# Seven products in place of eight for the second half of two squared-ReLU layers, and for three of four pairs of the first half

## The chip, the cores and the metric

The program runs on one core of one Trainium2 chip. The metric is the device time of one execution in microseconds (us). TensorE (PE in the rows; PEld is its weight loads) multiplies, VectorE (DVE), ScalarE (ACT) and GpSimd (POOL) do elementwise work, and SyncE (SP) issues the loads of weights.

## The reference, cut to what matters

Two blocks run one after the other on 512 tokens of 1024 channels, in float32. The first block is a gated delta rule with a SwiGLU layer, the second has two layers of attention, each followed by

```python
def sq_relu_mlp(x, w1, w2):
    h = jax.nn.relu(x @ w1)
    return (h * h) @ w2          # D_MODEL 1024, D_FF_2 4096

h = h + sq_relu_mlp(rms_norm(h, mlp_norm[i]), mlp_w1[i], mlp_w2[i])    # i = 0, 1
```

The change is in these two layers (`mlp`, called here mlp 0 and mlp 1). The SwiGLU layer (`w_gate_up` and `w_down`, 2816 wide) shares a helper with them.

## The kernel before

Everything is kept transposed: 128 channels on the partitions, tokens along the row. mlp 0 has 528 tokens, mlp 1 has 512; a half is 264 or 256. A product in float32 is made from three matmuls of split operands: high by high, high by low, low by high. Each weight tile `wr` is loaded by SP, copied to `wh` by ScalarE and subtracted to `wl` by VectorE; the splitting costs the two engines one instruction each.

**The helper `seven` (L104)** multiplies a 2x2 arrangement of weights by a 2x2 arrangement of operands with seven block products in place of eight. Four quarters of a pair of weight blocks arrive by four loads (L118 to L121); VectorE makes two sums of 128x512 (L122, L123) and GpSimd two more (L124, L125); the seven combinations are split in four groups (L130, L131: three of 128x1024, one of 128x512), and each product is 12 matmuls (L138), 84 in all. An object `evac` takes the results out of PSUM. The order is product 11, s2, s3, s1, 12, s4, 22; the last one adds to the bank of s3 after `out22` has read it.

**`mlp` (L1614)** works in four parts (`CHUNKS`) of eight feature blocks of 128. In a part, four pairs of feature blocks are made: in the first part two pairs by plain products (96 matmuls a pair), two by `seven`, in the later parts all four by `seven`, with `Squares` as evac. The features are ReLU, square and split to `fh` and `fl` (L177, L178). Then `down` (L1084) makes the eight output blocks by plain products of 8 blocks each (L1098) and `add` multiplies each result by the row of inverse norms `rs` and adds it to `h` (L1655, L1656). In mlp 0 `down` uses two halves of 264 columns, in mlp 1 one piece of 512. `operand_sums` (L1583) makes the summed operands t1 to t4 for the sevens in the first part.

**SwiGLU** uses `seven` for most of its second half, with the class `Adds` (L982) as evac: two runs of four sevens, and in each seven three of the six results go to `h` by a GpSimd addition (L1005, L1009, L1013).

Order is set by a scheduler that walks all instructions by priority and by its own estimate of time; each engine then runs its list in order, with semaphores between engines. A tile of a pool with `bufs=n` has n slots under its tag; a slot is free when everything that touches the tile in it is done. In `seven`, `wr` of g1 and g3 come from a pool with three slots (shared with the plain weights), g2 and g4 from another with two; `wh` and `wl` have two slots in each pool. PSUM has eight banks for `pd` in `mlp`.

## Time and profile before

| What | Value |
|---|---|
| median of 3 runs | 2571.34 us (2569.33 to 2573.19) |
| the profiled execution, its own time | 2559.74 us |
| its span | 2558.0 us |
| mean granted TensorE clock | 0.986 |
| busy share PE, DVE, ACT, POOL | 96%, 71%, 47%, 24% |

The time is that of the whole execution; the span runs from the first instruction to the last and is 1.74 us shorter. Matmuls are pipelined, so the busy share of PE counts their overlapping spans and is no measure of speed; the number of matmuls in a window is.

### The profile page before, as it was taken

What the parts mean: (1) busy time and instruction counts of PE and PEld (TensorE: products, weight loads), DVE (VectorE), ACT (ScalarE), POOL (GpSimd) and SP (SyncE); (2) the same over time, 40 slices, a digit from 0 to 9 for tenths busy, and PEclk for the clock granted to TensorE, in tenths of its full rate; (3) what the DMA queues carried; (4) which work ended last, traced back from release to release, by engine and by line L of the source; (5) the groups of instructions that cost most, each with busy time, mean ns of one, the idle gap of its engine ahead of it and who ended that gap; (6) DMA issues with size and microseconds to landing.
All of it is one profiled execution on the core that took longest, in us unless ns stands there. A gap on an engine that the chain in (4) does not pass through costs nothing.

```text
span 2558.0 us, 48433 instructions
## 1 busy us (share of the span) xinstructions
PE 2452.0 (96%) x18732; PEld 2306.2 (90%) x18732; DVE 1807.8 (71%) x3766; ACT 1203.1 (47%) x2419; POOL 607.5 (24%) x751
## 2 busy tenths in 40 slices
PE   8899999999999999999887999999999999999999
PEld 8899999999899888888887999999999999788987
DVE  7878877856654576655999667676764878866764
ACT  5434445343423333335455664543634767634543
POOL 2332222100001123232671220121121444301210
PEclk9999999999999999999998999999999999999999
DMA  4334342434563323233331323323333322223322
GB/s 155 96 98 106 86 115 80 110 96 117 173 231 96 91 78 112 85 95 108 93 77 34 94 92 95 104 79 96 119 106 92 106 64 75 86 94 107 104 90 92
DMA packets 150741, 257.36 MB, mean 101 GB/s; under 512 B 66816, under 2 KB 70944, under 8 KB 150512
## 3 DMA queue, kind: packets, MB, share of 16 engines
q1 hardware_dynamic: 93696, 236.47, 30.3%
q10 hardware_dynamic: 56816, 17.82, 3.6%
q8 instruction: 147, 2.41, 0.4%
q14 instruction: 82, 0.67, 0.1%
HBM read 223.39 MB, written 22.34 MB: 96 GB/s over the span
## 4 chain that ended last, share of the span: by engine, by line
PE 70%; DVE 15%; DMA 8%; ACT 3%; issue 3%; POOL 1%; SPq 0%; ACTq 0%; DVEq 0%; POOLq 0%
PE ps_pd L100 33%; PE ps_pd L1098 15%; PE ps_pd L138 8%; DMA wr<-wm 3%; DVE wl L131 2%; DVE wl L84 1%; PE ps_pa L1501 1%; PE ps_po L1945 1%; PE ps_pb L733 1%; DMA wd<-Xt 1%; DVE prod L910 1%; PE ps_pt L1934 1%; DVE sc L1430 1%; ACT wh L83 1%; DVE sc L1418 1%
## 5 line engine op out<-in xcount | busy, mean ns | idle before, releaser
L100 PE MATMUL ps_pd<-bigh,wh 128*128 128x256 f32 (+5 forms) x2256 | 693.6, 309 | 16.7 <-ACT bigh L180 6.4
L100 PE MATMUL ps_pd<-bigh,wl 128*128 128x256 f32 (+5 forms) x2256 | 691.6, 308 | 4.3 <-DVE wl L84 4.3
L100 PE MATMUL ps_pd<-bigl,wh 128*128 128x256 f32 (+5 forms) x2256 | 690.7, 307 | 0.9 <-DVE bigl L181 0.8
L83 ACT ACTIVATE wh<-wr 128x1024 fp32r<-128x1024 f32 (+3 forms) x295 | 302.7, 1027 | 549.6 <-PE ps_pd L100 230.8
L100 PEld LDWEIGHTS ps_pd<-bigh,wh 128*128 128x128 f32 (+1 forms) x2256 | 429.6, 191 | 37.9 <-ACT bigh L180 6.4
L100 PEld LDWEIGHTS ps_pd<-bigh,wl 128*128 128x128 f32 (+1 forms) x2256 | 429.3, 191 | 22.2 <-DVE wl L84 5.3
L100 PEld LDWEIGHTS ps_pd<-bigl,wh 128*128 128x128 f32 (+1 forms) x2256 | 429.2, 190 | 19.2 <-DVE bigl L181 1.6
L84 DVE TENSOR_TENSOR wl<-wr,wh 128x1024 fp32r<-128x1024 f32 (+3 forms) x283 | 348.1, 1230 | 88.6 <-ACT wh L83 83.8
L1098 PE MATMUL ps_pd<-fh,wh 128*128 128x264 f32 (+1 forms) x816 | 262.0, 326 | 1.9 <-ACT wh L83 1.8
L1098 PE MATMUL ps_pd<-fl,wh 128*128 128x264 f32 (+1 forms) x816 | 262.9, 325 | 0.0
L1098 PE MATMUL ps_pd<-fh,wl 128*128 128x264 f32 (+1 forms) x816 | 261.8, 326 | 0.1
L130 ACT ACTIVATE wh<-wr 128x1024 fp32r<-128x1024 f32 (+1 forms) x144 | 134.8, 950 | 179.2 <-DVE wr L123 67.5
L131 DVE TENSOR_TENSOR wl<-wr,wh 128x1024 fp32r<-128x1024 f32 (+1 forms) x144 | 177.5, 1244 | 13.2 <-ACT wh L130 12.3
L1098 PEld LDWEIGHTS ps_pd<-fh,wh 128*128 128x128 f32 x816 | 152.5, 188 | 17.1 <-ACT wh L83 4.5
L1098 PEld LDWEIGHTS ps_pd<-fh,wl 128*128 128x128 f32 x816 | 152.8, 188 | 13.6 <-DVE wl L84 0.6
L1098 PEld LDWEIGHTS ps_pd<-fl,wh 128*128 128x128 f32 x816 | 153.2, 188 | 13.0
L124 POOL TENSOR_TENSOR wr<-wr 128x512 f32<-128x512 f32 x36 | 58.2, 1617 | 437.4 <-DVE wr L122 256.9
L138 PE MATMUL ps_pd<-bigh,wh 128*128 128x264 f32 (+1 forms) x448 | 125.8, 285 | 5.9 <-DVE u L1563 4.3
L138 PE MATMUL ps_pd<-bigl,wh 128*128 128x264 f32 (+1 forms) x448 | 125.2, 283 | 1.2 <-DVE bigl L1594 1.2
L138 PE MATMUL ps_pd<-bigh,wl 128*128 128x264 f32 (+1 forms) x448 | 123.8, 282 | 0.0
L1655 DVE TENSOR_TENSOR y<-ps_pd,rrow 128x264 f32<-128x264 f32 (+1 forms) x96 | 49.1, 515 | 101.3 <-PE ps_pd L1098 95.2
L100 PE MATMUL ps_pd<-xh,wh 128*128 128x264 f32 (+1 forms) x400 | 116.3, 293 | 0.3 <-ACT t L1824 0.3
(517 smaller groups left out, 5881.9 us busy)
## 6 DMA issues: line engine op xcount, KB each, us to landing
wr<-w SPq DMA_DIRECT2D x72, 512.0 KB
wr<-wm SPq DMA_DIRECT2D x128, 256.0 KB
wr<-wm SPq DMA_DIRECT2D x64, 512.0 KB
wr<-wgu SPq DMA_DIRECT2D x44, 512.0 KB
wr<-wa SPq DMA_DIRECT2D x17, 512.0 KB
wr<-wkv SPq DMA_DIRECT2D x17, 512.0 KB
wr<-wdq SPq DMA_DIRECT2D x32, 256.0 KB
wr<-wao SPq DMA_DIRECT2D x16, 512.0 KB
```

The lines of the kernel that those rows point to most:

```text
L83: nc.scalar.activation(wh, wr, AF.Copy)
L84: (self.low or nc.vector).tensor_tensor(wl, wr, wh, ALU.subtract)
L100: nc.tensor.matmul(ps[:, :half], a[:, k], b[k][:, ts], start=(k == 0 and i == 0), stop=(k == kt - 1 and i == 2))
L124: nc.gpsimd.tensor_tensor(g1[:, 1], g2[:, 0], g4[:, 0], ALU.add)
L130: nc.scalar.activation(wh[:, : kq * m], v, AF.Copy)
L131: nc.vector.tensor_tensor(wl[:, : kq * m], v, wh[:, : kq * m], ALU.subtract)
L138: nc.tensor.matmul(ps, a[:, q], c[q], start=(start and q == 0 and i == 0), stop=(q == kq - 1 and i == 2), skip_group_check=not start,)
L733: nc.tensor.matmul(pq[r, c, :w], lhs(pr)[:, c], rhs(pr)[:, c], start=True, stop=True)
L910: nc.vector.tensor_tensor(prod[:, :i, :i], X[:, :i, :i], bt[:, :i, i].rearrange("p (o j) -> p o j", o=1).broadcast_to([2 * H, i, i]), ALU.mult
L1098: nc.tensor.matmul(pss[h][:, :half], a[:, q], b[f0 + q][:, ts], start=(f0 + q == 0 and i == 0), stop=(f0 + q == nf - 1 and i == 2),)
L1418: nc.vector.scalar_tensor_tensor(acc[:n, c0:c1], rl[:n, : c1 - c0], wi[:n, i, hd : hd + 1], acc[:n, c0:c1], ALU.mult, ALU.add)
L1655: nc.vector.tensor_tensor(y, ps, norm["rs"][:, t], ALU.mult)
```

## The change

The second half of both layers goes through `seven` too (16 calls in each `mlp`, with `Adds`), and in the three later parts the fourth pair of features is made by plain products. Since the operands of the second half now need sums of features, a class `Features` keeps seven blocks of half the tokens for a pair, `u`, and makes three differences and sums on VectorE. `h` is multiplied by the mean square (`inv`) in the first part and by the inverse (`rs`) in the last; the results of a product go into `h` without the norm row in between. For the first two outputs of a part `seven` runs with `last`: five products take their first three feature pairs before the fourth is needed. The slots move: g1, g3 and g4 come from the pool with three, g2 from a pool with one; the split of g4 has a tag of its own. The scratch tiles p1, u2 and w of `mlp` come from the tags `sq` and `acc` with two slots each, and so do those of `operand_sums`.

```diff
     def seven(self, wdram, x, n, evac, last=False):
-        pools = (self.wp, self.wq, self.wp, self.wq)
-        g1, g2, g3, g4 = (
-            p.tile([128, 2, 512], F32, name="wr", tag="wr", bufs=self.wr_bufs - (p is self.wq))[:, :, : kq * 128] for p in pools
-        )
+        def quarters(p, bufs):
+            return p.tile([128, 2, 512], F32, name="wr", tag="wr", bufs=bufs)[:, :, : kq * 128]
+
+        g1, g3, g4 = (quarters(self.wp, self.wr_bufs) for _ in range(3))
+        g2 = quarters(self.wq, 1)
...
+        both = ("wh", "wl")
+        groups = (
+            (("11", "s2"), (g1, 2, self.wp, both, self.ws_bufs)),
+            (("s3", "s1"), (g2, 2, self.wq, both, 1)),
+            (("12", "s4"), (g3, 2, self.wp, both, self.ws_bufs)),
+            (("22",), (g4, 1, self.wq, ("w3h", "w3l"), 1)),
+        )
...
+        tail = range(kq)
+        if last:
+            z = bank()
+            tail = range(kq - 1, kq)
+            for i in range(3):
+                weights(i)
+            for ps, w, b in ((x1, "11", "b11"), (u, "s2", "t2"), (y, "s3", "t3"), (v, "s1", "t1"), (z, "s4", "b22")):
+                product(ps, q[w], b, qs=range(kq - 1))
...
 class Adds:
-    def __init__(self, k, s, h, j, lo, half):
+    def __init__(self, k, scratch, h, j, lo, half, eng=None):
         self.k, self.nc, self.half = k, k.nc, half
-        self.p1, self.u2, self.w = (s.tile([128, half], F32, name=x, bufs=2) for x in ("p1", "u2", "w"))
+        self.eng = eng or k.nc.gpsimd
+        self.p1, self.u2, self.w = (scratch(x)[:, :half] for x in ("p1", "u2", "w"))
...
+class Features:
+    SLOTS = ("b11", "t3", "b21", "b22", "t1", "t2", "t4")
+    def __init__(self, k, s, m):
+        self.k, self.nc = k, k.nc
+        self.u = s.tile([128, 7, T // 2], F32, name="u", bufs=1)[:, :, :m]
+        self.parts = [s.tile([128, 7, T // 2], F32R, name=x, bufs=FPAIRS)[:, :, :m] for x in ("fh", "fl")]
...
+    def done(self, i):
+        k, nc, u, (hi, lw) = self.k, self.nc, self.u, self.parts
+        v = self.block(i)
+        nc.scalar.activation(v, v, AF.Square)
+        if i == 0:
+            k.split(hi[:, 0], lw[:, 0], u[:, 0])
+            nc.vector.tensor_tensor(u[:, 4], u[:, 0], u[:, 1], ALU.subtract)
+        else:
+            nc.vector.tensor_tensor(u[:, 1], u[:, 3], u[:, 1], ALU.subtract)
+            nc.vector.tensor_tensor(u[:, 5], u[:, 4], u[:, 3], ALU.add)
+            nc.vector.tensor_tensor(u[:, 6], u[:, 5], u[:, 2], ALU.subtract)
+            k.split(hi[:, 1:], lw[:, 1:], u[:, 1:])
...
 def operand_sums(k, h, x, norm, lo, n, i, scratch):
-    g22 = pool.tile([128, T // 2], F32, name="g22", tag="fh", bufs=RING)[:, :m]
+    g22 = scratch("p1")[:, :m]
...
 def mlp(k, io, h, i, before, lo=0, n=T):
+        def scratch(name):
+            if name == "w":
+                return k.sm.tile([128, 640], F32, name="w", tag="acc", bufs=2)
+            return k.sm.tile([128, T], F32, name=name, tag="sq", bufs=2)
...
         for c in range(CHUNKS):
+            fs = []
+            for j in range(part // 2):
+                w = w1[(i * nf + c * part) // 2 + j]
+                fs.append(Features(k, s, m))
+                if j in MIX[min(c, 1)]:
+                    k.seven(w, x, n, Squares(k, scratch, m, fs[-1]))
                 else:
+                    plain(w, fs[-1])
...
+                row("inv", k.sm.tile([128, T], F32, name="inv", tag="sq", bufs=2), ms)
+            y = {c: tuple([f.parts[e][:, a] for f in fs] for e in range(2)) for a, c in enumerate(Features.SLOTS)}
+            for j in range(0, 8, 2):
+                v = h[:, j : j + 2, tokens]
+                if c == 0:
+                    nc.gpsimd.tensor_tensor(v, v, rows["inv"].rearrange("p (o t) -> p o t", o=1).broadcast_to(list(v.shape)), ALU.mult)
+                end = c == CHUNKS - 1
+                late = end and j == 6
+                k.seven(w2[i, j // 2, c], y, n, Adds(k, scratch, h, j, lo, m, nc.vector if late else None), j == 0)
...
+                if end:
+                    for a in range(2):
+                        (nc.vector if late else nc.gpsimd).tensor_tensor(v[:, a], v[:, a], rows["rs"], ALU.mult)
+
+MIX = ((2, 3), (0, 1, 2))
+FPAIRS = 4
...
-RING = 10
```

## Rows read from the trace of the kernel before

**Rows 1.** The page: span, and busy us (share) xinstructions of each engine.

```profile
span 2558.0 us, 48433 instructions
PE 2452.0 (96%) x18732; PEld 2306.2 (90%) x18732; DVE 1807.8 (71%) x3766; ACT 1203.1 (47%) x2419; POOL 607.5 (24%) x751
```

**Rows 2.** Windows at full pace: SwiGLU sevens, mlp 0 `down`, mlp 1 `down`.

```profile
1080.00:1090.00 10.00, 10.00 (x87) 10.00 (x86) 6.14 (x11) 3.00 (x4) 6.00 (x4) 1.00 0.38 107
...
1680.00:1700.00 20.00, 20.00 (x166) 20.00 (x165) 14.87 (x22) 6.09 (x7) 4.31 (x3) 1.00 0.25 83
...
2360.00:2380.00 20.00, 20.00 (x88) 16.28 (x87) 13.42 (x16) 4.77 (x5) 4.71 (x3) 1.00 0.20 66
```

**Rows 3.** Windows: first part, later parts of mlp 0 and 1, one SwiGLU seven.

```profile
1529.60:1603.00 73.40, 71.28 (x570) 69.80 (x569) 54.71 (x104) 31.80 (x54) 7.15 (x4) 1.00 0.28 88
...
1732.50:1821.20 88.70, 88.45 (x723) 88.03 (x722) 62.08 (x93) 39.18 (x56) 14.64 (x8) 1.00 0.29 90
...
2420.60:2506.60 86.00, 84.74 (x531) 75.78 (x530) 57.62 (x77) 38.89 (x56) 14.19 (x8) 1.00 0.29 92
...
959.70:971.20 11.50, 10.20 (x85) 10.03 (x85) 9.43 (x12) 4.04 (x6) 8.60 (x6) 1.00 0.39 115
```

**Rows 4.** PE's waits (us, times, longest): SwiGLU sevens, mlp 0, mlp 1.

```profile
PE ps_pd L138 <- DVE p L1004: 4.7, 3, 1.9
...
PE ps_pd L138 <- DVE u L1563: 1.5, 3, 0.8
...
PE ps_pd L138 <- DVE u L1563: 2.8, 3, 1.1
```

**Rows 5.** Groups of VectorE by shape in mlp 0: busy us, mean ns.

```profile
L131 DVE TENSOR_TENSOR wl<-wr,wh 128x1024 fp32r<-128x1024 f32 x41 | 57.2, 1406 | 5.9 <-ACT wh L130 5.3
...
L178 DVE TENSOR_TENSOR fl<-u,fh 128x528 fp32r<-128x528 f32 x30 | 22.2, 740 | 15.6 <-ACT fh L177 15.5
...
L123 DVE TENSOR_TENSOR wr<-wr 128x512 f32<-128x512 f32 x13 | 9.0, 691 | 7.2 <-DMA wr<-wm 7.0
L122 DVE TENSOR_TENSOR wr<-wr 128x512 f32<-128x512 f32 x13 | 8.9, 688 | 12.5 <-DMA wr<-wm 12.2
L131 DVE TENSOR_TENSOR wl<-wr,wh 128x512 fp32r<-128x512 f32 x13 | 8.8, 678 | 0.0
...
L1563 DVE TENSOR_TENSOR u<-ps_pd,w 128x264 f32<-128x264 f32 x14 | 6.0, 431 | 0.4
...
L1594 DVE TENSOR_TENSOR bigl<-gt,bigh 128x264 fp32r<-128x264 f32 x8 | 3.1, 418 | 0.0
```

**Rows 6.** Timeline of VectorE in a SwiGLU seven (start us, us).

```profile
969.65 0.69 DVE L123 TENSOR_TENSOR wr<-wr 128x512 f32<-128x512 f32 x1 [1.88 <-DMA wr<-wdq]
...
975.27 1.43 DVE L131 TENSOR_TENSOR wl<-wr,wh 128x1024 fp32r<-128x1024 f32 x1
...
976.96 0.89 DVE L131 TENSOR_TENSOR wl<-wr,wh 128x512 fp32r<-128x512 f32 x1
```

**Rows 7.** Timeline of SP's issues in the same stretch: g4 of two sevens.

```profile
966.32 0.33 SPq L119 DMA_DIRECT2D wr<-wdq  x1
...
977.88 0.33 SPq L119 DMA_DIRECT2D wr<-wdq  x1
```

**Rows 8.** Timelines: VectorE and GpSimd, overlapping and alone.

```profile
1621.25 3.46 DVE L131 TENSOR_TENSOR wl<-wr,wh 128x1024 fp32r<-128x1024 f32 x2 [0.38 <-ACT wh L130]
...
1624.97 1.21 DVE L131 TENSOR_TENSOR wl<-wr,wh 128x1024 fp32r<-128x1024 f32 x1
...
1592.21 1.29 POOL L125 TENSOR_TENSOR wr<-wr 128x512 f32<-128x512 f32 x1 [4.77 <-DMA wr<-wm]
...
1621.30 2.33 POOL L125 TENSOR_TENSOR wr<-wr 128x512 f32<-128x512 f32 x1
...
982.06 0.74 POOL L1009 TENSOR_TENSOR h<-h,w 128x256 f32<-128x256 f32 x1 [0.70 <-DVE w L1008]
```

**Rows 9.** Timeline of VectorE at the end of the span.

```profile
2554.20 0.69 DVE L1656 TENSOR_TENSOR h<-h,y 128x512 f32<-128x512 f32 x1
```

More of the change, by code (lines that the diff above doesn't have):

```diff
@@ L101, in products, with seven @@
             evac(ps[:, :half], slice(h * half, (h + 1) * half))
-    def seven(self, wdram, x, n, evac):
+    def seven(self, wdram, x, n, evac, last=False):
         nc = self.nc
@@ L132, in part, with product @@
             return [(wh[:, kq * i : kq * i + kq], wl[:, kq * i : kq * i + kq]) for i in range(m)]
-        def product(ps, w, b, start=True):
+        def product(ps, w, b, start=True, qs=range(kq)):
             (wh, wl), (bh, bl) = w, x[b]
-            for q in range(kq):
+            for q in qs:
                 for i, (a, c) in enumerate(((wh, bh), (wh, bl), (wl, bh))):
@@ L144, in bank @@
             return self.pst("pd")[:, :half]
-        groups = ((0, g1, 2), (1, g2, 2), (2, g3, 2), (3, g4, 1))
+        both = ("wh", "wl")
[5 more added lines that the diff above has]
+        )
         q = {}
         def weights(i):
-            q.update(zip((("11", "s2"), ("s3", "s1"), ("12", "s4"), ("22",))[i], part(*groups[i])))
+            q.update(zip(groups[i][0], part(*groups[i][1])))
         x1, u, y, v = bank(), bank(), bank(), bank()
-        weights(0)
-        product(x1, q["11"], "b11")
+        tail = range(kq)
[7 more added lines that the diff above has]
+        else:
+            weights(0)
+        product(x1, q["11"], "b11", qs=tail)
         evac.first(x1)
-        product(u, q["s2"], "t2")
+        product(u, q["s2"], "t2", qs=tail)
         evac.second(u)
-        weights(1)
-        product(y, q["s3"], "t3")
-        product(v, q["s1"], "t1")
+        if not last:
+            weights(1)
+        product(y, q["s3"], "t3", qs=tail)
+        product(v, q["s1"], "t1", qs=tail)
         evac.third(v)
-        weights(2)
+        if last:
+            product(z, q["s4"], "b22", qs=tail)
+        else:
+            weights(2)
         product(x1, q["12"], "b21", start=False)
@@ L165, in seven @@
         evac.out22(y)
-        z = bank()
-        product(z, q["s4"], "b22")
+        if not last:
+            z = bank()
+            product(z, q["s4"], "b22")
         evac.out12(z)
@@ L1672, in mlp @@
-        for c in range(CHUNKS):
-            f = [[s.tile([128, T], F32R, name=x_, bufs=RING) for x_ in ("fh", "fl")] for _ in range(part)]
-            for j in range(0, part, 2):
-                w = w1[(i * nf + c * part + j) // 2]
-                if c == 0 and j < 2 * PLAIN:
-                    plain(w, f[j : j + 2])
-                    for e in range(4 // PLAIN * (j // 2), 4 // PLAIN * (j // 2 + 1)):
-                        operand_sums(k, h, x, f"mnorm{i}", lo, n, e, s)
-                else:
-                    k.seven(w, x, n, Squares(k, s, n, f[j : j + 2]))
-                if c == 0 and j == 2 * PLAIN:
+                for a, qt in enumerate(quarters):
+                    nc.sync.dma_start(wr[:, 4 * a : 4 * a + 4], w[:, qt])
@@ new lines, in mlp @@
+        for c in range(CHUNKS):
+            fs = []
[4 more added lines that the diff above has]
+                    k.seven(w, x, n, Squares(k, scratch, m, fs[-1]))
+                else:
+                    plain(w, fs[-1])
+                if c == 0 and j < PLAIN:
+                    for e in range(4 // PLAIN * j, 4 // PLAIN * (j + 1)):
+                        operand_sums(k, h, x, f"mnorm{i}", lo, n, e, scratch)
+                if c == 0 and j == PLAIN:
```

97 lines of the change are left out of this document (46 added, 51 removed).

## The prediction

> **What bounds the kernel now.** I read the page first, then windows of 20 us over the two layers, the waits of PE there, the groups of VectorE, and last the timelines of a run of sevens. The page shows PE at 96% and VectorE at 71% [rows 1]; both are means over stages, so I look at the layers alone. In full windows PE starts 166 matmuls of 264 columns in 20 us, 88 of 512 columns in 20 us, and 87 of 256 columns in 10 us [rows 2]: 0.1205, 0.2273 and 0.115 us each. (A window counts those that straddle its ends, so these prices are a little low, all of them alike.) A later part of mlp 0 has 4 x 84 + 8 x 48 = 720 matmuls, 86.8 us at that price, and took 88.7; a later part of mlp 1 has 336 of 256 columns and 192 of 512, 82.3 us, and took 86.0 [rows 3]. So TensorE sets the pace with 2 to 4 us of waits and small losses in a part. VectorE is busy 62.1 of the 88.7 us and ScalarE 39.2 [rows 3]: VectorE has 27 us to spare in a part, and that reserve is what the change spends.
>
> The reader should look next at where PE does wait. In mlp 0 and mlp 1 the longest sum is a wait for L1563, the reading of bank y by `out22`, 1.5 and 2.8 us in three times each, and in SwiGLU the same instruction of `Adds`, L1004, 4.7 us in three times over two runs of four sevens [rows 4]. The timeline says why: VectorE runs in order, and in front of the evacuation stands L123, which waited 1.88 us for the load of g4 [rows 6]. That load is issued (977.88) when the split of the previous g4 is over (976.96 + 0.89) [rows 6, 7], and L123 of the one before began 3.3 us after its issue (966.32 to 969.65). So in a run of sevens the chain is: sums, four splits, load of the next g4, sums. Its period is the 11.56 us between the two issues [rows 7], while PE needs 84 x 0.115 = 9.7 us. The runs of four in `mlp` suffer little because the plain `down` in front gives the loads time to run ahead.
>
> **The change part by part.**
>
> *Matmuls removed.* Each of 16 pairs of outputs of a layer goes from 96 matmuls of half width to 84, and three pairs of features from 84 to 96. mlp 0: (-192 + 36) x 0.1205 = -18.8 us. mlp 1: the 768 matmuls of 512 columns (174.6 us) become 1344 of 256 (154.6), -20.0, and 36 x 0.115 = +4.1: -15.9. Together -34.7 us if PE stays the bound. A later part would need 684 x 0.1205 = 82.4 us in mlp 0 and 78.7 in mlp 1.
>
> *Work added on VectorE.* A seven for features: two sums 0.69 each, splits 3 x 1.41 + 0.68, five readings of PSUM at 0.43: 8.4 + the new features. These were two splits of 0.74; they become four additions and one split of 264 at 0.42 and one split of 1584, which by the step from 512 (0.68) to 1024 (1.21 undisturbed) is 1.8: 3.9 us in all [rows 5, 8]. Sum 12.3 us. A plain pair: two splits of 1.41 and 3.9: 6.7. A seven with `Adds`: the window of one such seven has 9.43 us busy [rows 3]. A later part: 3 x 12.3 + 6.7 + 4 x 9.4 = 81.2 us. That is 99% of PE's 82.4 us in mlp 0, and more than its 78.7 in mlp 1: VectorE goes from a reserve to a second bound. ScalarE gains splits too but has half of a part free [rows 3].
>
> *Where the overload falls.* In the three sevens for features VectorE needs 2.2 us more than PE's 10.1, 6.6 us in a row; the plain pair behind them gives back 11.6 - 6.7 = 4.9. What can be put off is the second half of the features, about 3.1 us, but only up to the next `out11`, since `u` has one slot. Nothing of it costs time if it fits (0), and all of it if nothing can be put off (6.6). I take 2.5 in a part, on the side of the deferral: x6 = +15.
>
> *The longer run.* A later part now has seven sevens in a row (four outputs, then three features), then a plain pair. Four of the followers (three outputs and the first features) are like SwiGLU's, which pay 4.7 us over six followers, 0.8 each [rows 4]; 3.2 in a part if nothing else changes. But the slots move: the first slot free in the pool of three is that of g1, and the next g4 can take it, so the late load becomes the one behind the third split, at 975.27 + 1.43 = 976.70 in place of 977.85 [rows 6], 1.15 us earlier against a lateness of 1.88. Bounds 0 and 3.2, I take half, 1.6, less the 0.5 and 0.9 that a part of today pays for L1563 [rows 4]: about +0.9, x6 = +5.
>
> *First parts.* `operand_sums`, the squares, p1 and u2, and for a time `inv`, now share two slots of `sq`; before, `operand_sums` had ten. Four rounds of sums that overlapped must go one behind the other, and `inv` holds one of the two slots until GpSimd has made its four multiplications of two rows, each at least 2 x 1.29 us [rows 8]: 10.3 us in which u2 of the first output has no slot unless it got one earlier. A late u2 stops `second`, then `out22`, then product 22; PE can work ahead in three further banks for about 4.3 us. So between 0 and 6 us in each layer. Today's first part has 73.4 - 71.3 = 2.1 us without PE [rows 3]; I take +3, x2 = +6.
>
> *Nearly free.* The GpSimd additions and multiplications hide behind PE, with 8.6 of 11.5 us busy in a seven of outputs [rows 3]; the 2.6 us of `rs` that the last part adds to a seven would fill it, and that is a reason for the upper end. The first output of a part no longer needs the last pair at once: `last` gives 45 matmuls, 5.4 us, for a chain of about 6 us; even. The tail replaces 0.69 + 0.69 us after the last matmul [rows 9] by two half additions and a 0.69 us product: +0.2. SwiGLU's own eight sevens get the new slots: 0 within 2 us either way, taken as 0.
>
> *Sum.* -34.7 + 15 + 5 + 6 + 0.2 = -8.5 us; the profiled 2559.7 us becomes 2551. The median of the runs shown lies 11.6 us higher, and the same step from it gives 2563 us.
>
> **GpSimd against VectorE.** Two splits beside GpSimd took 3.46 us, one alone 1.21, and GpSimd's sum 2.33 beside them, 1.29 undisturbed [rows 8]. The Trainium skill, "SBUF — State Buffer", section "Who interferes with whom", says that a VectorE instruction with two SBUF inputs and a GpSimd instruction that reads SBUF exclude each other for the whole instruction. By that rule this trace's undisturbed durations would simply add up, and the sum would be +6 in place of -8.5 (third rival).
>
> **The rivals.**
> 1. *The saving is kept* (chance 0.15). The deferral works and the slots end the late loads: -35 us, 2537. For it: PE's floor still lies above VectorE's in mlp 0. Against: 99% on an engine that idles 2 us in each period for a load [rows 3, 6].
> 2. *The run of sevens sets the period* (0.2; the other side). If the followers keep SwiGLU's 11.5 us and those with features take VectorE's 12.3, a later part is 10.1 + 3 x 11.5 + 3 x 12.3 + 11.6 = 93.1 us in place of 88.7, and 92.1 in place of 86.0 in mlp 1: 3 x 4.4 + 3 x 6.1 = +31; the first parts gain about 1: 2601 us. It decides from an average follower of 11.2 us in mlp 0 and 10.9 in mlp 1, above which the part is longer than today. For it: it is the period that the trace shows [rows 7]; against: the slots, and the plain pair in which loads run ahead.
> 3. *The two engines take turns* (0.15). A seven of outputs has 5.7 us of VectorE work with two inputs in SBUF (0.69 x 2 + 3 x 1.21 + 0.68) and 2 x 1.29 + 3 x 0.74 = 4.8 of GpSimd, each undisturbed [rows 5, 8]: 10.5 us, 0.4 above PE in mlp 0 and 0.8 in mlp 1, x 4 sevens x 3 parts = +14 on my sum: +6, 2577 us. Against: in the window of one seven VectorE was busy 9.43 us and idle about 2 [rows 3], so 10.5 us of turns did not fit there without overlap.
>
> **How the numbers follow.** My sum has 0.37, the rivals 0.15, 0.2 and 0.15; 0.13 is spread over both sides. The range goes from just above the first rival to short of the second, 2540 to 2595, and leaves out about one in ten at each end; the sum alone, with its bounds, spans 2545 to 2575. About 0.2%, 5.1 us, is what can be told from no change. Faster: most of my sum, the first rival and a little of the rest, 0.50. Slower: second rival, most of the third, and the rest, 0.32. Same: 0.18.
>
> **What would show it.** Parts of mlp 0 at 85 to 88 us and VectorE busy above 78 in them; PE waits for `out22` and `wl` of 3 to 5 us in a part; in the first part a wait behind u2 or a bank. If VectorE is idle where PE waits, the loads are the cause and not its load; if parts fall to 83 us, the first rival holds. I am wrong if followers average above 11.2 us, or if the order chosen by the scheduler puts something else in front, such as `last` waiting for three groups of weights at once.

## The result, and the profile after

The changed kernel takes 2724.53 us (median of four runs, 2722.20 to 2736.26) against 2570.34 us of the kernel before, measured beside it: 1.0612 times as long, 95% interval 1.0576 to 1.0649. The prediction was 2563, its range 2540 to 2595. The page of the profile after, its span, the engines and the granted clock in 40 slices, answers to [rows 1]:

```profile
span 2723.8 us, 50183 instructions
...
PE 2489.8 (91%) x19198; PEld 2359.9 (87%) x19198; DVE 1994.1 (73%) x3980; ACT 1272.2 (47%) x2507; POOL 842.2 (31%) x913
...
PEclk9899999999999999999799889999899999799998
```

The span grew by 165.8 us. PE has its 19,198 matmuls, 35 us less work at the prices of [rows 2], and yet is busy 37.8 us longer; GpSimd has 235 us more. Windows of the four parts of mlp 0, each cut at the same place of the code as in [rows 3] (length, then busy us of PE, PEld, DVE, ACT and POOL, each with its instructions in brackets, then the granted clock):

```profile
1520.70:1624.80 104.10, 73.64 (x514) 70.06 (x513) 81.99 (x107) 42.22 (x69) 54.16 (x33) 0.85 0.17 56
1624.80:1724.20 99.40, 88.28 (x684) 85.66 (x684) 78.85 (x107) 46.96 (x67) 39.84 (x27) 0.98 0.26 85
1724.20:1825.60 101.40, 90.00 (x684) 87.39 (x684) 78.53 (x108) 47.08 (x68) 39.86 (x27) 0.95 0.25 84
1825.60:1938.30 112.70, 95.73 (x696) 92.63 (x696) 92.60 (x122) 56.92 (x81) 46.16 (x33) 0.92 0.30 99
```

The first part went from 73.4 to 104.1 us, the middle parts from 88.7 to 99.4 and 101.4, the last to 112.7. A middle part has the 684 matmuls that were foretold, 82.4 us of work. TensorE's waits over the whole span, four of the longest sums and one more (L141 is the matmul of `seven`; us in all, times, longest):

```profile
PE ps_pd L141 <- ACT wh L133: 34.2, 30, 2.8
PE ps_pd L141 <- DVE fl L201: 22.2, 6, 4.3
PE ps_pd L141 <- DVE p L1028: 19.9, 17, 3.0
PE ps_pd L141 <- ACT fh L200: 17.8, 7, 10.2
...
PE ps_pd L141 <- DVE wl L134: 10.8, 13, 3.1
```

SwiGLU's share of these is 1.5 us. Before, the longest sum in one of the two mlp layers was 2.8 us [rows 4]; in the changed mlp 0 alone that for `wh` is 21.7 us. Three places stand behind these rows.

**The run of sevens.** VectorE from one seven to the next, in the third part of mlp 0:

```profile
1810.03 0.69 DVE L125 TENSOR_TENSOR wr<-wr 128x512 f32<-128x512 f32 x1 [2.25 <-issue]
...
1812.71 4.04 DVE L134 TENSOR_TENSOR wl<-wr,wh 128x1024 fp32r<-128x1024 f32 x2
...
1817.35 1.21 DVE L134 TENSOR_TENSOR wl<-wr,wh 128x1024 fp32r<-128x1024 f32 x1
...
1818.83 0.90 DVE L134 TENSOR_TENSOR w3l<-wr,w3h 128x512 fp32r<-128x512 f32 x1
1821.91 0.69 DVE L125 TENSOR_TENSOR wr<-wr 128x512 f32<-128x512 f32 x1 [2.18 <-DMA wr<-wm]
```

and SP's issue of the first quarter's load (L123) in between:

```profile
1818.58 0.33 SPq L123 DMA_DIRECT2D wr<-wm  x1
```

The period is 11.9 us. From the first sum (L125) to the end of the third split VectorE has no gap: 1810.03 to 1818.56. The next load of g1 is issued at 1818.58, when that split has given its slot back, and the next L125 starts 3.3 us later, after 2.18 us in which VectorE idled. It is the chain of [rows 6, 7], with one link changed.

**From the last features to the first output.** VectorE and ScalarE at the end of the second part's features:

```profile
1674.26 0.69 DVE L125 TENSOR_TENSOR wr<-wr 128x512 f32<-128x512 f32 x1 [1.46 <-DMA wr<-wm]
...
1676.00 1.75 DVE L126 TENSOR_TENSOR wr<-wr 128x512 f32<-128x512 f32 x1
...
1677.68 1.80 DVE L201 TENSOR_TENSOR fl<-u,fh 128x1584 fp32r<-128x1584 f32 x1
...
1679.51 1.24 ACT L1705 ACTIVATE u<-ps_pd 128x264 f32<-128x264 f32 x4 [4.79 <-DVE fl L201]
...
1684.95 1.81 DVE L201 TENSOR_TENSOR fl<-u,fh 128x1584 fp32r<-128x1584 f32 x1 [1.65 <-ACT fh L200]
```

The split of the third pair's features (L201 at 1677.68) stands behind two sums (L125, L126) and a split for the next seven. ScalarE's Relu of the plain pair (L1705) waited 4.79 us for it, since `u` has one slot; the plain pair's own features then follow, until 1686.76. The plain pair's matmuls (L100, 1658.95 to 1672) had run before the last product of the third pair's seven was over, so nothing was left to cover the wait. In windows of 10 us:

```profile
1550.00:1560.00 10.00, 3.73 (x17) 3.73 (x18) 8.32 (x6) 2.66 (x4) 6.02 (x4) 0.50 0.17 57
1660.00:1670.00 10.00, 10.00 (x84) 10.00 (x83) 9.29 (x12) 5.93 (x9) 4.37 (x2) 1.00 0.17 60
1670.00:1680.00 10.00, 6.42 (x51) 6.21 (x50) 7.18 (x9) 4.26 (x6) 2.79 (x2) 0.98 0.26 90
1680.00:1690.00 10.00, 8.26 (x51) 7.45 (x49) 6.16 (x11) 6.63 (x11) 0.61 (x1) 0.85 0.00 0
...
1720.00:1730.00 10.00, 8.33 (x69) 8.12 (x68) 8.24 (x12) 3.98 (x5) 7.04 (x5) 1.00 0.20 71
```

The first row is from the first part, for the clock (last section). Then come 84 matmuls in the plain pair, 51 and 51 on the way, and 69 in a window of the next run of sevens.

**The first part.** TensorE's two longest waits there, and GpSimd's multiplication of h by the inverse mean square beside three instructions of VectorE:

```profile
PE ps_pd L265 <- POOL acc L257: 10.9, 1, 10.9
PE ps_pd L141 <- ACT fh L200: 10.2, 1, 10.2
```

```profile
1563.96 11.48 POOL L1744 TENSOR_TENSOR h<-h,inv 128x1056 f32<-128x1056 f32 x4 [7.74 <-ACT inv L1716]
```

```profile
1564.95 2.43 DVE L1738 TENSOR_TENSOR rcol<-rcol 128x5 f32<-128x5 f32 x1
...
1567.65 2.69 DVE L201 TENSOR_TENSOR fl<-u,fh 128x264 fp32r<-128x264 f32 x1
...
1573.10 2.89 DVE L125 TENSOR_TENSOR wr<-wr 128x512 f32<-128x512 f32 x1
```

The squares for the norm came 11 us late, and then the four multiplications (11.48 us) lay beside VectorE, four of whose five instructions on two SBUF operands took 2.4 to 2.9 us meanwhile: a split of 264 columns 2.69, where the same split took 0.43 at 1682.54 in the next part. The features behind it were late by 10.2 us. In the first part of mlp 1 the two longest waits are 11.5 us (for L1606) and 9.3 us (for `rcol`).

### The profile page after: what moved, and what is told of

Same layout as the page of the kernel before. It is cut to its first block, busy times and chain, and to the rows that moved or that the text cites. A ratio compares the mean times of both kernels' runs of the same rounds, so it can differ in the third digit from the quotient of the medians.

```text
span 2723.8 us, 50183 instructions
## 1 busy us (share of the span) xinstructions
PE 2489.8 (91%) x19198; PEld 2359.9 (87%) x19198; DVE 1994.1 (73%) x3980; ACT 1272.2 (47%) x2507; POOL 842.2 (31%) x913
## 5 line engine op out<-in xcount | busy, mean ns | idle before, releaser
L100 PE MATMUL ps_pd<-bigh,wh 128*128 128x256 f32 (+5 forms) x2256 | 695.0, 309 | 18.8 <-ACT bigh L203 6.3
L100 PE MATMUL ps_pd<-bigh,wl 128*128 128x256 f32 (+5 forms) x2256 | 692.2, 308 | 2.9 <-DVE wl L84 2.9
L100 PE MATMUL ps_pd<-bigl,wh 128*128 128x256 f32 (+5 forms) x2256 | 691.3, 307 | 2.7 <-DVE bigl L204 2.4
L100 PEld LDWEIGHTS ps_pd<-bigh,wh 128*128 128x128 f32 (+1 forms) x2256 | 430.1, 191 | 40.9 <-ACT bigh L203 6.5
L100 PEld LDWEIGHTS ps_pd<-bigl,wh 128*128 128x128 f32 (+1 forms) x2256 | 429.9, 191 | 22.3 <-DVE bigl L204 5.0
L100 PEld LDWEIGHTS ps_pd<-bigh,wl 128*128 128x128 f32 (+1 forms) x2256 | 430.0, 191 | 20.9 <-DVE wl L84 3.7
L84 DVE TENSOR_TENSOR wl<-wr,wh 128x1024 fp32r<-128x1024 f32 (+3 forms) x231 | 281.6, 1220 | 87.8 <-ACT wh L83 84.4
L133 ACT ACTIVATE wh<-wr 128x1024 fp32r<-128x1024 f32 x186 | 189.4, 1052 | 247.6 <-DVE wr L126 88.6
L141 PE MATMUL ps_pd<-fl,wh 128*128 128x256 f32 (+1 forms) x960 | 279.4, 295 | 22.4 <-DVE fl L201 22.2
L141 PE MATMUL ps_pd<-fh,wh 128*128 128x256 f32 (+1 forms) x960 | 272.3, 296 | 28.4 <-ACT fh L200 17.8
L134 DVE TENSOR_TENSOR wl<-wr,wh 128x1024 fp32r<-128x1024 f32 x186 | 259.1, 1408 | 24.9 <-ACT wh L133 24.6
L141 PE MATMUL ps_pd<-fh,wl 128*128 128x256 f32 (+1 forms) x960 | 269.1, 294 | 3.6 <-DVE wl L134 3.5
L127 POOL TENSOR_TENSOR wr<-wr 128x512 f32<-128x512 f32 x62 | 103.7, 1673 | 383.0 <-DVE wr L125 332.3
L141 PEld LDWEIGHTS ps_pd<-fh,wh 128*128 128x128 f32 x960 | 186.9, 199 | 34.6 <-ACT fh L200 19.4
L141 PEld LDWEIGHTS ps_pd<-fl,wh 128*128 128x128 f32 x960 | 192.3, 200 | 24.4 <-DVE fl L201 24.0
L141 PEld LDWEIGHTS ps_pd<-fh,wl 128*128 128x128 f32 x960 | 186.7, 200 | 5.2 <-DVE wl L134 4.9
L100 PE MATMUL ps_pd<-xh,wh 128*128 128x264 f32 (+1 forms) x592 | 171.5, 292 | 5.5 <-ACT h L1823 5.2
L100 PE MATMUL ps_pd<-xl,wh 128*128 128x264 f32 (+1 forms) x592 | 170.1, 289 | 0.0
L100 PE MATMUL ps_pd<-xh,wl 128*128 128x264 f32 (+1 forms) x592 | 169.3, 290 | 0.0
L128 POOL TENSOR_TENSOR wr<-wr 128x512 f32<-128x512 f32 x62 | 103.7, 1672 | 59.4 <-DMA wr<-wm 35.0
L100 PEld LDWEIGHTS ps_pd<-xh,wh 128*128 128x128 f32 x592 | 114.0, 193 | 6.4 <-ACT h L1823 5.4
```

The source lines that it names most:

```text
L84: (self.low or nc.vector).tensor_tensor(wl, wr, wh, ALU.subtract)
L100: nc.tensor.matmul(ps[:, :half], a[:, k], b[k][:, ts], start=(k == 0 and i == 0), stop=(k == kt - 1 and i == 2))
L127: nc.gpsimd.tensor_tensor(g1[:, 1], g2[:, 0], g4[:, 0], ALU.add)
L128: nc.gpsimd.tensor_tensor(g3[:, 1], g1[:, 1], g3[:, 0], ALU.add)
L133: nc.scalar.activation(wh[:, : kq * m], v, AF.Copy)
L134: nc.vector.tensor_tensor(wl[:, : kq * m], v, wh[:, : kq * m], ALU.subtract)
```

## The experiments

"The run" below is the time from the second output seven of a middle part to the last seven of features of the part behind it: five followers, that is sevens right behind another one, taken by ScalarE's reading of the first bank (`first`). In the changed kernel it is 58.8 us (1692.0 to 1750.8), 11.8 a follower. From that last one to the first `first` of the outputs ("the way over") it is 34.4 us. Both are of mlp 0. Each ratio is to the kernel before, measured beside it, with its 95% interval; the changed kernel has 1.0612.

**e1: one sum from GpSimd to VectorE.**

```diff
-        nc.gpsimd.tensor_tensor(g1[:, 1], g2[:, 0], g4[:, 0], ALU.add)
+        nc.vector.tensor_tensor(g1[:, 1], g2[:, 0], g4[:, 0], ALU.add)
```

> One sum of the weights (g1's second quarter) is made by VectorE in place of GpSimd; everything else is the changed kernel (2724.5 us). Theory A, the chain of loads: in the middle parts a seven has a period of 11.5 us because its chain is third split, load of g1 (3.2 us), first sum (0.69), GpSimd sum (1.75), copies and splits; with the GpSimd sum replaced by 0.69 us on VectorE the chain is 1.0 us shorter, a period of about 10.5, a middle part 100 -> 94 us, the whole about 2690. Theory B, VectorE is full: it has 79 us of work in a part of 100 and gets 7 x 0.7 = 5 us more, so periods grow to about 12, the whole to about 2750.

2743.1 us, 1.0687 [1.0620, 1.0754], near theory B's 2750. The run stayed at 58.9 us. The step through GpSimd could be taken out of the chain and the chain stayed as long: VectorE paid what GpSimd gave up.

**e2: the plain pair first, then the three sevens.**

```diff
-MIX = ((2, 3), (0, 1, 2))
+MIX = ((2, 3), (1, 2, 3))
```

> In the later parts the plain pair is the first of the four in place of the last (MIX (1, 2, 3)). Theory A: the gap of 4 to 5 us and the one of 1.5 us behind it at the start of the second products come from two chains of features one behind the other, since u has one slot and PE had pulled the plain pair's matmuls into the seven before; with a seven last only one chain of about 7 us stands against 5.4 us of matmuls, the gaps fall from 6 to about 2 us a part, the whole by 25 us to about 2700. Rival: the gap belongs to the three groups of weights that the first seven of the second product wants at once; then it stays as it is, 2724 within 6.

2770.9 us, 1.0795 [1.0739, 1.0851]; neither theory foretold a loss. TensorE's waits for weights (`wh`) rose to 31.0 us in mlp 0 from 21.7. A reading of it, not tested by itself: without a plain pair behind the sevens nothing pays off what they owe.

**e3: without the multiplications of h** by the inverse mean square and by `rs` (left out; h is not normalised).

```diff
-                if c == 0:
-                    nc.gpsimd.tensor_tensor(v, v, rows["inv"].rearrange("p (o t) -> p o t", o=1).broadcast_to(list(v.shape)), ALU.mult)
...
-                if end:
-                    for a in range(2):
-                        (nc.vector if late else nc.gpsimd).tensor_tensor(v[:, a], v[:, a], rows["rs"], ALU.mult)
```

> Leaves out the multiplications of h by inv (first part) and by rs (last part). Theory A: in the first part they hold GpSimd for 11.5 us while VectorE's instructions with two inputs in SBUF take 2.4 to 2.9 us each, and PE waits 10 us for the last features; in the last part they lengthen three sevens by 2 to 3 us each; so the first parts get 10 us shorter and the last parts 8, the whole about 2688. Rival: the first part is held by the shared slots of sq (squares, operand sums, p1, u2) and the last part by its VectorE work; then less than 10 us in all is gained, about 2715.

2704.5 us, 1.0536 [1.0466, 1.0607]: between the two, some 20 us (0.0076 of 2566) less than the changed kernel, though the intervals touch. The wait for the features in the first part fell from 10.2 to 3.0 us, that for the squares stayed at 10.5. VectorE's four stretched instructions (2.43, 2.69, 2.56 and 2.89 us) take 0.16, 0.43, 0.69 and 0.69 here: 8.6 us less, against 7.2 less of wait.

**e4: the kernel before with the changed slots of the seven** (three tiles in the pool of three, one in that of one).

```diff
-        pools = (self.wp, self.wq, self.wp, self.wq)
...
+        g1, g3, g4 = (quarters(self.wp, self.wr_bufs) for _ in range(3))
+        g2 = quarters(self.wq, 1)
```

> The kernel before (2570 us) with the slots of the changed seven alone: g1, g3 and g4 from the pool of three, g2 and each split from pools of one; the second products stay plain. Theory A: the run of sevens has the same chain with either set of slots, so SwiGLU's two runs and the runs of four in both layers change by less than 1 us each, 2570 within 6. Rival: the new slots themselves make the runs slow, since nothing can be loaded ahead; then each of the eight runs of the two layers loses 4 us or more, and SwiGLU 2 each, 2600 or above.

2584.3 us, 1.0064 [1.0044, 1.0084]. Neither theory: the waits in SwiGLU fell (`p` 1.4 us in place of 4.7), but mlp paid, `wl` 9.3 and `wh` 7.5. The slots alone lose some 16 us (0.0064 of 2566); they were no relief.

**e5 and e9: slots for the squares.** In e5 a slot of their own in place of the shared `sq`; in e9 two of its own for the scratch tile w, which frees `acc`, and the squares move there. The edit of e9, cut:

```diff
-                return k.sm.tile([128, 640], F32, name="w", tag="acc", bufs=2)
+                return p.tile([128, T // 2], F32, name="w", bufs=2)
...
-                    acc = k.squares(tiles(h), lo=lo, eng=nc.gpsimd)
+                    acc = k.accumulator(k.sm, lo)
...
+                            sq = k.sm.tile([128, 640], F32, name="sqn", tag="acc", bufs=2)
```

> The squares for the norm get a slot of their own in place of the two that they share with the operand sums, p1 and u2. Theory A (the 11 us in which TensorE waits in each first part for the accumulator of the squares come from those two shared slots): the squares run beside the operand sums again, the wait falls below 3 us in each first part, 2724 becomes about 2704. Rival B (the squares' additions are late because GpSimd has too much queued in front of them): the wait stays at 8 us or more and the time at 2718 to 2726.

2735.3 us, 1.0661 [1.0553, 1.0768]: no gain, the wait for the squares stayed at 11.2 us, and theory A fell. GpSimd's timeline in e5:

```profile
1534.12 0.19 POOL L237 MEMSET acc<- 128x112 f32 x1 [0.35 <-DVE bigl L1646]
1537.55 1.74 POOL L1739 TENSOR_TENSOR acc<-acc,sqn 128x528 f32<-128x528 f32 x1 [3.24 <-ACT acc L1735]
```

The accumulator's memset waited for L1646, which reads the last operand sum w: the slot that was missing is that of the accumulator (`acc`), which w shares.

> In the run with a slot of its own for the squares they started as late as before, since their accumulator shares two slots with the sum w of the operand sums. Here w gets two slots of its own, and accumulator and squares have the two slots of acc for themselves. Theory A (that slot makes the 11 us in which TensorE waits for the squares in each first part): the squares run beside the operand sums, the wait falls below 3 us, about 20 us less, 2704. Rival B (VectorE's and GpSimd's queues at that point are full in any case, so that the first output's features come as late): the wait goes, and the next one grows by the same amount, 2718 to 2730.

2706.7 us, 1.0554 [1.0499, 1.0609]. TensorE's waits in the first part of e9:

```profile
PE ps_pd L141 <- DVE fl L201: 7.7, 1, 7.7
PE ps_pd L141 <- ACT fh L200: 4.5, 1, 4.5
PE ps_pd L141 <- ACT wh L133: 3.9, 3, 1.9
PE ps_pd L276 <- DVE ms L1742: 3.6, 1, 3.6
```

Theory A's 2704. The wait of 10.9 us for the squares is gone, one of 3.6 for their mean (`ms`) is left, and that for the features (7.7 and 4.5) stayed. By the two ratios some 15 us are gained over both layers, though their intervals touch.

**e6: slots for the loads to run ahead** (on e3, g4 with two slots of its own).

```diff
-        g1, g3, g4 = (quarters(self.wp, self.wr_bufs) for _ in range(3))
+        g1, g3 = (quarters(self.wp, self.wr_bufs) for _ in range(2))
+        g4 = self.wq.tile([128, 1, 512], F32, name="w4", tag="w4", bufs=2)[:, :, : kq * 128]
```

> On top of the kernel without the multiplications of h by the inverse mean square and by rs (2704.5, both left out here as well, and the row rs with them), the fourth quarter's weights get two slots of their own, so that the loads of the first and third quarter have a slot to run ahead. Theory A (the run of sevens has a period of 11.5 to 11.9 us because 8.5 us of VectorE's work and a load of 3.3 us stand one behind the other): the period falls to about 10.3 us, seven sevens in six parts and two in two save 1.2 us each, 2704 becomes about 2650. Rival B (VectorE's own work beside GpSimd sets the period): the idle time of VectorE goes, but its instructions get longer, the period stays above 11.2 us and the time above 2690.

2705.6 us, 1.0545 [1.0432, 1.0658], as e3: rival B's numbers, though not its reason, since VectorE still idles for a load. The run fell only to 57.6 us, and the way over grew to 39.1 (1750.0 to 1789.1), where e3 has 34.0. SP's issue of g2, and the sum that waits for it:

```profile
1797.17 0.33 SPq L122 DMA_DIRECT2D wr<-wm  x1
```

```profile
1800.93 0.69 DVE L126 TENSOR_TENSOR wr<-wr 128x512 f32<-128x512 f32 x1 [2.09 <-DMA wr<-wm]
```

g2 has one slot, and its load took the place of that of g1 in the chain: 3.8 us from issue to sum. One slot more moved the wait to the next tile; why the way over grew was not looked at.

**e7: outputs read older features** (those of the first two pairs twice, the last two unread).

```diff
-            y = {c: tuple([f.parts[e][:, a] for f in fs] for e in range(2)) for a, c in enumerate(Features.SLOTS)}
+            y = {c: tuple([f.parts[e][:, a] for f in (fs[:2] * 2)] for e in range(2)) for a, c in enumerate(Features.SLOTS)}
```

> The products of the outputs read the features of the first two pairs twice and leave the last two pairs unread, so that no output waits for the pair just made; all other work stays. Theory A (the way from the last features to the first output of a part costs 6 to 7 us in each of eight parts, and the first parts a further wait behind the features): about 50 us less, 2675. Rival B (the work that VectorE owes at that point is only put off, and the wait comes back in the sevens behind): 2710 or more.

2695.0 us, 1.0504 [1.0420, 1.0587]; between the two. The way over fell from 34.4 to 26.3 us, the run grew to 59.9.

**e8 and e18: none and two of four pairs of features by seven** in the later parts (e8 as below, e18 with `(0, 1)`).

```diff
-MIX = ((2, 3), (0, 1, 2))
+MIX = ((2, 3), ())
```

> The later parts make all four pairs of features by two products, as the first parts make two of theirs; the first parts stay. A later part then has 720 matmuls in units of half the tokens, as before the change. Theory A (the price is in the runs of sevens and in the way from the features to the outputs, so in the arrangement): three followers at 11.6 in place of 10.1 us, and about 4 us behind the features, 86.8 + 4.5 + 4 = 95 us in place of 99 to 101 in mlp 0, about 2695. Rival B (VectorE's load is the price: 81 us of work in a part): VectorE has 65 us to do, parts fall to the 88.9 us of before, 2655.

> The complete kernel with two of the four pairs of features of each later part by seven, in place of three. With three it takes 2724, with none 2691. Theory A (each seven of features leaves VectorE the same debt, and a run of sevens the same price for each): about 2713. Rival B (the debt of two is paid off by the two plain pairs behind them, and only the third is too many): 2695 or less.

e8: 2690.6 us, 1.0487 [1.0366, 1.0608], theory A. e18: 2695.9 us, 1.0504 [1.0483, 1.0525], rival B. Two cost no more than none, within the intervals, though they have 24 matmuls less in a part, and the third some 28 us (1.0612 less 1.0504): two sevens and two plain pairs balance, three and one don't. But four fifths of the loss, 0.0487 of 0.0612, are there without any of these sevens, with as many matmuls in a later part as before.

**e10: without the sums of weights** (left out; the second halves of the tiles are loaded).

```diff
-        nc.sync.dma_start(g2[:, 1], wd[:, 3])
+        nc.sync.dma_start(g1, wd[:, 0:2])
+        nc.sync.dma_start(g2, wd[:, 2:4])
+        nc.sync.dma_start(g3, wd[:, 1:3])
...
-        nc.sync.dma_start(g1[:, 0], wd[:, 0])
-        nc.sync.dma_start(g3[:, 0], wd[:, 2])
-        nc.vector.tensor_tensor(g2[:, 0], g2[:, 1], g1[:, 0], ALU.add)
-        nc.vector.tensor_tensor(g2[:, 1], g2[:, 1], g4[:, 0], ALU.add)
-        nc.gpsimd.tensor_tensor(g1[:, 1], g2[:, 0], g4[:, 0], ALU.add)
-        nc.gpsimd.tensor_tensor(g3[:, 1], g1[:, 1], g3[:, 0], ALU.add)
```

> Leaves out the four sums of weights of every seven (two on VectorE, two on GpSimd): the second halves of the three tiles are loaded in their place, so that the splits stay, and a split waits for its load alone. Theory A (the chain of sums, splits and a load in series sets the 11.5 us of the run of sevens): followers at 10.2 to 10.5 us in mlp 0, 1.2 us for some 52 of them and 0.8 for SwiGLU's, about 2655. Rival B (what costs is the first parts, the last parts and the way from the features to the outputs): the period falls, PE waits there for longer, 2695 or more.

2595.1 us, 1.0119 [1.0063, 1.0175]: of the loss 0.0493 is gone, 126 us, far more than theory A's 70. The window of the run in the changed kernel, and in e10:

```profile
1692.00:1750.80 58.80, 52.73 (x418) 51.13 (x417) 46.28 (x62) 23.87 (x33) 30.39 (x21) 1.00 0.27 89
```

```profile
1665.60:1716.00 50.40, 50.40 (x416) 50.40 (x415) 36.70 (x55) 24.89 (x33) 13.48 (x11) 1.00 0.61 196
```

58.8 us became 50.4, 10.1 a follower, which is PE's own 84 x 0.1205 us, at a full PE. ScalarE's splits there:

```profile
1765.64 1.06 ACT L129 ACTIVATE wh<-wr 128x1024 fp32r<-128x1024 f32 x1 [0.89 <-PE ps_pd L137]
1768.56 1.06 ACT L129 ACTIVATE wh<-wr 128x1024 fp32r<-128x1024 f32 x1 [1.86 <-PE ps_pd L137]
```

They wait for PE to give weights back, not for a load or a sum. In mlp 1 a run loses more: 2482.2 to 2547.2 in the changed kernel is 65.0 us for 455 matmuls, 52.3 us of work at the price of [rows 2]; in e10 47.5 us hold 404 (2391.0 to 2438.5), 46.5 us of work. How the 126 us divide among the runs, the ways over, the first and last parts and SwiGLU was not separated.

**e13, e14, e16: what of the sums it is.** e13 keeps every sum in its place, over 16 columns (the rest loaded); e14 makes them in full, each behind the split of its tile; e16 leaves out GpSimd's two.

```diff
-        nc.vector.tensor_tensor(g2[:, 0], g2[:, 1], g1[:, 0], ALU.add)
...
+        nc.vector.tensor_tensor(g2[:, 0, t], g2[:, 1, t], g1[:, 0, t], ALU.add)
```

with `t = slice(0, 16)` and all four alike in e13, and in e14, over tiles loaded whole:

```diff
             q.update(zip(groups[i][0], part(*groups[i][1])))
+            g = groups[i][1][0]
...
+                eng.tensor_tensor(g[:, 1], g[:, 1], g[:, 0], ALU.add)
```

> The four sums of weights stand where they stood, but are made over 16 columns in place of 512 (the other columns are loaded), so that every wait of the chain stays and its work is gone. Theory A (the order load, sum, split and the slots set the period, whatever the sums take): 2675 or more. Rival B (the sums' work on VectorE, and on GpSimd beside it, is the price): 2600, as without the sums.

> All four sums of 512 columns are made, on the same engines, but each behind the split of its tile, over loaded weights, so that no split waits for a sum. Theory A (the order is the price): 2610, VectorE as busy as in the changed kernel. Rival B (the work is): 2690 or more. In between, near 2650, both.

> GpSimd's two sums of every seven are left out (their tiles are loaded whole), VectorE's two stay. Theory A (VectorE's time and its wait for the loads make the chain, as the run with the third sum on VectorE said): 2690 or more. Rival B (the step through GpSimd, 1.3 to 2 us for a sum, and VectorE's splits that are longer beside it, are most of the price): 2640 or less.

e13: 2668.4 us, 1.0384 [1.0354, 1.0414], between its theories and nearer to A. e14: 2694.4 us, 1.0485 [1.0455, 1.0515], rival B's number. e16: 2700.2 us, 1.0508 [1.0477, 1.0538], theory A's. The run in e13, e14 and e16:

```profile
1687.40:1743.50 56.10, 53.48 (x424) 51.77 (x423) 37.56 (x64) 24.37 (x33) 17.23 (x21) 1.00 0.50 167
```

```profile
1678.40:1738.40 60.00, 54.09 (x417) 51.28 (x416) 46.55 (x62) 23.30 (x32) 26.34 (x21) 1.00 0.50 160
```

```profile
1693.10:1750.20 57.10, 54.08 (x436) 53.04 (x435) 39.95 (x62) 24.83 (x33) 12.75 (x11) 1.00 0.45 147
```

In e13 VectorE has nearly as little to do as in e10 (37.6 us, there 36.7), and still a follower takes 11.2 us. It idles for the load of g1, which SP issued at the end of the third split (1793.73 + 1.21); first VectorE's two sums and that split, then the issue:

```profile
1788.88 0.17 DVE L126 TENSOR_TENSOR wr<-wr 128x16 f32<-128x16 f32 x1 [1.10 <-DMA wr<-wm]
...
1793.73 1.21 DVE L135 TENSOR_TENSOR wl<-wr,wh 128x1024 fp32r<-128x1024 f32 x1
...
1800.01 0.18 DVE L126 TENSOR_TENSOR wr<-wr 128x16 f32<-128x16 f32 x1 [3.90 <-DMA wr<-wm]
```

```profile
1794.96 0.33 SPq L123 DMA_DIRECT2D wr<-wm  x1
```

So the period is a sum of two terms. From a sum (1788.88) to the end of the third split (1794.94) VectorE needs 6.1 us, where the changed kernel needs 8.5; then the load takes 5.05 us, where there it takes 3.3, since it brings both halves of g1 here: 11.1 us against 11.9. That longer load is a flaw of e13, and of e16, which loads the same way: there the load of g1 took 4.7 us (1804.03 to 1808.72), VectorE was busy 40.0 us in place of 46.3, and the run still took 57.1. With e13's 6.1 us and the shorter load of 3.3 the chain would come to 9.4 us, an estimate, less than PE's 10.1: by that estimate it would do for PE to set the pace if the chain were 1.8 us shorter. No run with the sums in place shows it. e14 did not cut the order as meant. The split no longer waits for the sum, but the slot does, as GpSimd's sum and SP's next issue into the tile show:

```profile
1799.66 1.29 POOL L159 TENSOR_TENSOR wr<-wr 128x512 f32<-128x512 f32 x1 [2.16 <-issue]
```

```profile
1800.98 0.33 SPq L121 DMA_DIRECT2D wr<-wm  x1
```

The sum ends at 1800.95, the issue follows at 1800.98. A sum in the life of a tile holds back its next load, in front of the split or behind it. The run of e14 is even longer, 60.0 us; where it gains its 30 us was not looked at, and it decides nothing between its two theories. A version with all sums and with slots for a second seven's loads wasn't tried, and no run shows whether SBUF has room for it beside `fh`, `fl` and `u`.

**e11: without GpSimd's additions to h** (three of the four blocks of an output seven are not added).

```diff
-        self.eng.tensor_tensor(self.h22, self.h22, self.p1, ALU.subtract)
...
-        self.eng.tensor_tensor(self.h12, self.h12, self.w, ALU.add)
...
-        self.eng.tensor_tensor(self.h21, self.h21, self.u2, ALU.subtract)
```

> Leaves out the three additions to h that end each seven of outputs in mlp (on GpSimd, 0.74 us each undisturbed; the one to h11 on VectorE stays). Theory A (the two engines exclude each other, and each addition of GpSimd is paid by VectorE in full): 2.2 us less for VectorE in each of 32 sevens of outputs, the period there from 11.7 to about 10, the time 2670. Rival B (the additions fit beside VectorE's readings of PSUM and its idle 2 us in a period): within 12 us of the changed kernel, 2712 to 2730.

2708.9 us, 1.0563 [1.0510, 1.0615]. The run fell to 56.9 us. Near B: some 13 us by the ratios, whose intervals touch, a small part of the price.

**e12: four suspects at once** (the edits of e3, e7, e8 and e9).

> All four suspects away at once: accumulator and squares with their own slots, no multiplications of h by the inverse mean square and by rs (left out), outputs that read the features of the first two pairs twice (the last two left unread), and no features by seven products in the later parts. Theory A (they are separate delays, so that the savings measured alone add: 20 for the multiplications, 30 for the features, 34 for the sevens of features, and what the slot gives): about 2625. Rival B (they hide one another, one engine's load stands behind all): above 2650. Before has as many matmuls in these parts, so what is left above it, 55 us by A, is the price of the runs of four sevens.

2660.4 us, 1.0374 [1.0322, 1.0426]. B. The waits hide one another in part, and what these four leave is the chain of weights: in mlp 0 the longest sum of waits is `wh`, 16.3 us.

**e15: the kernel before without its sums.**

> The kernel before without its sums of weights, the second halves loaded as in the run without sums of the changed kernel. If the sums cost only where sevens follow one another (theory A), before gains what SwiGLU's two runs of four and its few waits in mlp show, 5 to 15 us: 2555. If each seven pays for its sums (rival B), 36 sevens in place of 60 gain 60% of 130 us: 2490. By A the changed kernel without sums stays about 40 us above this one.

2557.2 us, 0.9959 [0.9937, 0.9981]. A: 11 us. Sums cost next to nothing where a seven has plain products behind it, and 126 us in the changed kernel, where seven of them stand in a row.

**e17: nothing in the way** (the edits of e3, e7, e9 and e10).

> The sums of weights left out, and with them the multiplications of h by the inverse mean square and by rs; the squares and their accumulator with slots of their own; the outputs read the features of the first two pairs twice and leave the last two unread. All matmuls, splits, loads and features stay. Theory A (sums, first parts, last parts and the way from the features to the outputs are all that stood between the saving of matmuls and the time): 2595 less 18, 20 and 30, so about 2527, some 30 us below the kernel before without its sums (2557). Rival B (a further price, such as the clock or the half-width matmuls themselves): 2555 or more.

2535.3 us, 0.9874 [0.9855, 0.9893]. A. Two middle parts of mlp 0 in e17, from `first` to `first`:

```profile
1640.70:1724.20 83.50, 83.50 (x687) 83.50 (x686) 63.43 (x94) 48.00 (x67) 13.63 (x12) 1.00 0.51 168
1724.20:1807.40 83.20, 83.20 (x686) 83.20 (x685) 63.05 (x94) 47.89 (x66) 15.65 (x12) 1.00 0.52 168
```

83.5 and 83.2 us with PE full throughout, against 82.4 of the prediction's price. The first of them is 6.3 us to the second `first`, 50.4 of run and 26.8 of way over, where the changed kernel has 7.2, 58.8 and 34.4, together 100.4. A middle part before took 88.7 us [rows 3]: what the matmuls save does appear once everything in their way is gone. e17 as a whole lies 22 us below e15, but it leaves out more than e15 does, so these 22 us are not a measure of the matmuls' 35. No complete kernel with the change comes near the one before; even without any sums (e10 against e15) the change is some 40 us behind (1.0119 against 0.9959).

## Why the prediction was wrong

*Matmuls, -35.* Right as a price of TensorE (a middle part of e17 takes 83.5 and 83.2 us, 82.4 were foretold), and worth nothing: TensorE did not set the pace.

*The longer run, +0.9 a part.* This step failed first. The late load did move to the slot behind the third split, as foretold, but the 1.15 us that it comes earlier were taken to end half of the lateness, and SwiGLU's 0.8 us a follower was halved. Measured: 11.8 us a follower in place of 10.1, 8.4 us in five followers, and past the 11.2 that the prediction itself had named as the sign of being wrong. The sevens of features pay it too: 13.9 and 10.9 us for the two followers that make outputs, then 10.9, 13.3 and 9.7 for those that make features. The 0.8 us came from the waits in SwiGLU's runs of four [rows 4], ahead of which plain products let the weights run in advance; a wait appears only when that lead is used up. The period in [rows 7], 11.56 us against 9.7, was there to be used.

*VectorE's overload, +2.5 a part.* The work was sized well (81.2 us foretold, 78.9 measured in 99.4), its meaning not. VectorE was not full: in the run it idled 2.2 us in each period for a load, and it was busy 46.3 of 58.8 us. Its work counts there as a term of the period, beside the wait for weights, and not as a load that fills it. Only the third seven of features, too many for the plain pairs behind it, was near to what this step meant: 28 us (e18).

*`last`, "even".* The way over costs 34.4 us where e17 takes 26.8: 7.6 us in each part. Without the sums, of which two stand in front of the features' split, it is 30.0 us (e10); with outputs that don't wait for the last features it is 26.3 (e7). That two pairs' features go one behind the other because `u` has a single slot is read from the timeline (ScalarE's 4.79 us); no run gave `u` a second one.

*First parts, +3 each.* The window has 514 matmuls, 61.9 us of work, and took 104.1. Shared slots were named as the mechanism and that was right, but the wrong slot (`sq`; it was `acc`, e5 and e9), and what was priced was one late tile (3 us), where all the squares behind it came late: 10.9 us. The multiplications on GpSimd were priced by their own 10.3 us (11.48 measured) as a slot held; what they did was to stretch VectorE, by 8.6 us in four instructions (e3).

*`rs`, "nearly free".* The last part is 11 to 13 us longer than a middle one. e3 gave back some 20 us in all. In mlp 0 of its trace 7.3 us of that lie in the first part, from the last `first` of the features to that of the first output (16.2 us in place of 23.5), and 6.0 in the last part, from the first output to the fourth (38.3 in place of 44.3).

*Rivals.* The second had the mechanism, load and VectorE in series, with 93.1 us for a part against 99.4 to 101.4: right for the run, and without the way over, the first and the last parts. The third is partly so. The Trainium skill, "SBUF — State Buffer", section "Who interferes with whom", has a VectorE instruction with two SBUF inputs and a GpSimd instruction that reads SBUF exclude each other for the whole instruction. The 2.69 us for a split of 264 beside GpSimd's multiplications agrees. In the run, taking GpSimd's sums away (17.6 us busy less, e16) shortened VectorE's unchanged instructions by 6.3 us: there about a third was paid, not the whole; how much of the rest fell beside readings of PSUM or idle time was not looked at.

*What was not foreseen* is the granted clock. Busy time times mean clock fell by 32.4 us (2452.0 x 0.986 to 2489.8 x 0.958, an estimate), about the 35 us of work taken away, so PE's 37.8 us more of busy time is for the most part the lower level. Short breaks add to it: in the run, at full clock, 418 matmuls, 50.4 us of work, show as 52.73 us busy. No term of the sum stood for the clock.

## What to carry to other kernels

Where a stage has the form load, combine, split, multiply, look at how long a tile holds its slot: here the period of a run of them was the engine's work from the first use to the release plus the load (8.5 + 3.3 us, and 6.1 + 5.05 in e13), with VectorE busy 79% of the run. A short run between other work hides it, so a wait measured in a run of four says little of a run of seven; take the period. And before a scratch tile is put into a shared slot, ask what else takes that slot, and on whose queue the one that comes too late stands.

## What the runs showed of the hardware that was not expected

The granted clock fell to the lower of its two levels (1.2 in place of 2.4 GHz) after one long wait of TensorE, and not after shorter ones. In the windows above the clock is 0.50 in 1550 to 1560, in which PE is busy 3.73 us around a wait of 10.9 us, and 0.85 in 1680 to 1690, behind a wait of 3.6 us; it is 1.00 in 1720 to 1730, where PE stood 1.67 us at once, and in the whole run from 1692.0 to 1750.8, where it stood 6.1 us in all and never longer than 1.7. Matmuls behind such a gap started 0.22 us apart and later 0.12. Over the span the mean fell from 0.986 to 0.958, and rose to 0.972 in e10 and 0.977 in e17. A long wait is thus paid twice; how much of the 165.8 us of span is the second payment was not measured by itself.
